# A diffusion layer's FFN stage: gate 2's rows in two f32r passes, columns summed by squares of 32 on VectorE, normed features moved by way of DRAM

## The chip, the cores and the metric

One core of a Trainium2 chip runs the whole layer in one launch. Its engines are TensorE (PE, matrix products and transposes into PSUM), VectorE (DVE), ScalarE (ACT), GpSimd (POOL) and SyncE (SP, which issues every DMA of this kernel). Each engine takes its instructions in a fixed order and waits on semaphores for the others. The metric is the time of one execution on the device, in microseconds (us).

## The reference

One layer over 256 latent tokens and 256 context tokens of width 2048. What matters here is the second half and the modulation that goes into it:

```python
sh1, sc1, g1, sh2, sc2, g2 = split(silu(c) @ w_ada + b_ada, 6)     # w_ada: 2048 x 12288
...
x = layer_norm(DN_ALPHA * x + g1 * (heads @ w_out), ln1_g, ln1_b)
u = x * (1 + sc2) + sh2
x = layer_norm(DN_ALPHA * x + g2 * ((silu(u @ w_gate) * (u @ w_up)) @ w_down), ln2_g, ln2_b)
```

w_gate and w_up are 2048 x 5632, w_down is 5632 x 2048, all f32. The 256 tokens are two tiles of 128 rows.

## The kernel before

**Products.** A large f32 product is made of three f32r products (mm3, lines 274 to 276): the weights are split into hi (an f32r copy by ACT, L264 or L498) and lo (raw minus hi by DVE, L265 or L501), the activations likewise, and hi x hi, lo x hi and hi x lo are summed. A 1 MB piece of weights lies in one of four raw buffers (load_raw, L244); it is split in two halves of 1024 columns, and four hi and four lo buffers hold them. A raw buffer comes free when DVE has made both lo halves, a hi or lo buffer when PE has used it.

**Modulations.** Most parts of silu(c) @ w_ada are summed on DVE: ada_vector_steps loads w_ada by pieces, and vector_sum (L384) adds each piece, times the value of c of its partition, into a tile adav of 128 partitions. What is left is the sum over the 128 partitions. Where the result is wanted as a row on all partitions (gate 2, g2sb), rows_from (L394) multiplies a 128x128 matrix of ones with the 512 columns in f32 and ACT copies the bank (L395). Where it is wanted as a column per feature (shift sh2 and scale sc2 of the second modulation), each 128 columns are the stationary side of an f32 matmul with two columns of ones (second_columns_of, L995, eight for 512 shifts and 512 scales; second_scales, L1291, four for 512 scales). DVE then writes sh2 and sc2, and combine (L988 to L990, POOL) makes of them and of the layer norm's gain and shift the two columns mA and mB per feature.

The 16 feature blocks of 128 form four groups of four. Group 0 is summed on DVE and placed in the planned part; group 1's shifts are summed on PE (L1270) and its scales on DVE (scales, placed by second_scales); groups 2 and 3 are summed on DVE (side, second_modulation).

**Normed rows.** normalise (L1068, DVE) leaves (x - mean) times 1/deviation in xt, tokens on the partitions. The FFN's product wants features on the partitions. z_part (lines 1326 to 1337) does this for two feature blocks: four 128x128 transposes on PE (L1330), two ACT scalings by mA and mB out of PSUM into uf (L1334), an ACT copy to u2h (L1336), and a DVE subtraction to u2l (L1337). Group 0 goes by z_flip and z_rest (L1303, L1449 to L1452) for each token tile; groups 1, 2 and 3 take two z_part each.

**Order.** Up to the end of the first layer norm the order is planned by a small scheduler written in the kernel (Flow) and, with a stretch after it, lies in a hand-ordered region (manual_schedule): each engine takes the region's instructions in the order of the program. The stretch holds the first FFN products and ends with normalise for the column groups 1 to 3. After the region the compiler's scheduler orders each engine by what is ready, earlier code first; it may put later instructions into gaps of the region.

**The first half of the FFN.** There are 11 hidden blocks of 512. For the first ten the products over the early feature groups are made before the rest and kept in spill tiles: blocks 0 to 2 over group 0 (one step for gate and one for up), blocks 3 to 9 over groups 0 and 1 (two steps each). A step (project) is one 1 MB piece of weights and 24 matmuls. first_half lists the steps: steps 0 and 1 (block 0) lie in the region as first_products; step 2 is block 1's gate, step 3 its up, steps 4 and 5 block 2, step 6 block 3's gate over group 0, step 7 the same over group 1, and so on. The scales' steps are merged with steps 3 to 5; then group 1 is combined and placed (combine(1), z_part(4), z_part(6)); then the steps from 6 on are merged with side; the last two steps follow the placing of groups 2 and 3. After that every block is finished in turn over its missing groups, activated (activate), turned by DVE in squares of 32 x 32 (squares, L1375), put to a DRAM scratch by four DMAs of 64 KB (put, L1380), read back by one of 256 KB (get, L1385), which moves the squares across the partitions, and split (place). The down projection follows, with gate 2's rows merged into it: ada_rows is used by gate2_steps, once per 512 columns.

## Time and profile before

| | |
|---|---|
| median of 3 runs | 1145.33 us (1141.98, 1145.33, 1145.77) |
| the profiled execution | 1143.35 us |
| its span, first to last instruction | 1141.5 us |
| granted TensorE clock, mean | 0.996 |
| instructions | 14234 |
| DMA | 321.28 MB, mean 281 GB/s |

Times of the trace are counted from the span's start. The FFN's first product starts at 396, the placing of group 1 lies at 432 to 439, that of groups 2 and 3 at 579 to 586, and gate 2's first row at 912. In lists of groups a line reads: line, engine, operation, output<-inputs, shapes, count | busy us, mean ns of one | idle time of the engine before them and what ended it. In the chain and the timeline a line reads: start, length, what, with the idle time before it in brackets. An f32 matmul shows as two records, an f32r matmul as one. "busy" of PE overlaps from one matmul to the next, since they are pipelined.

### The profile page before, as it was taken

The numbers are of one execution on the slowest core, as the hardware profiler recorded it, in microseconds if no ns is written. First come the engines' busy times: TensorE is split into PE (matmuls) and PEld (weight loads), VectorE is DVE, ScalarE is ACT, GpSimd is POOL, SyncE is SP. The second block draws the span as 40 slices with busy tenths as digits, with TensorE's granted clock in tenths as the row PEclk, the third lists the DMA queues.
The fourth block names the chain that finished last, engine by engine and source line by source line (L and its number), as shares of the span: only waits on it lengthen the run. The fifth ranks groups of instructions, "written<-read, shape, count | busy, mean of one in ns | idle before, by whom it ended". The sixth has DMA issues, their size and how long they took to land.

```text
span 1141.5 us, 14234 instructions
## 1 busy us (share of the span) xinstructions
PE 1120.3 (98%) x5347; PEld 905.3 (79%) x5347; DVE 829.0 (73%) x1053; ACT 546.6 (48%) x784; POOL 41.8 (4%) x82
## 2 busy tenths in 40 slices
PE   8999999999999999999999999999999999999995
PEld 8766678787878788888888888888888888888884
DVE  4753579899998897767767566776766787676556
ACT  3332454886784355444464444444444344333341
POOL 1000040110100000010000000000000000000000
PEclk9999999999999999999999999999999999999998
DMA  8999999786999878989876776677677888877531
GB/s 266 393 359 404 389 374 343 256 269 211 344 343 366 314 268 318 328 302 316 306 213 228 232 240 226 220 252 258 207 263 239 312 313 332 318 272 261 197 131 74
DMA packets 186270, 321.28 MB, mean 281 GB/s; under 512 B 8620, under 2 KB 51020, under 8 KB 183895
## 3 DMA queue, kind: packets, MB, share of 16 engines
q1 hardware_dynamic: 186200, 320.36, 80.7%
q8 instruction: 42, 0.69, 0.2%
q14 instruction: 28, 0.23, 0.1%
HBM read 304.07 MB, written 16.25 MB: 281 GB/s over the span
## 4 chain that ended last, share of the span: by engine, by line
PE 93%; DVE 4%; DMA 1%; ACT 1%; issue 1%; SPq 0%; DVEq 0%; ACTq 0%
PE acc L274 28%; PE acc L276 27%; PE acc L275 27%; PE wk L549 2%; PE wk L942 2%; DMA raw<-in_w_ada_dram 1%; PE wk L1133 1%; DVE g1b L384 1%; PE wk L274 1%; PE wk L276 1%; PE wk L275 1%; PE wk L636 1%; PE wk L995 0%; DVE lo L501 0%; DVE xt L1537 0%
## 5 line engine op out<-in xcount | busy, mean ns | idle before, releaser
L265 DVE TENSOR_TENSOR lo<-raw,hi 128x1024 fp32r<-128x1024 f32 x258 | 312.3, 1220 | 184.2 <-ACT hi L264 180.9
L264 ACT CAST hi<-raw 128x1024 fp32r<-128x1024 f32 x258 | 271.0, 1055 | 343.5 <-PE acc L276 302.6
L274 PE MATMUL acc<-hi,u2h 128*128 128x512 f32 x704 | 274.6, 390 | 1.4 <-ACT u2h L1451 1.4
L276 PE MATMUL acc<-hi,u2l 128*128 128x512 f32 x704 | 274.1, 389 | 0.0
L275 PE MATMUL acc<-lo,u2h 128*128 128x512 f32 x704 | 274.0, 389 | 0.0
L274 PEld LDWEIGHTS acc<-hi,u2h 128*128 128x128 f32 x704 | 132.2, 188 | 29.6 <-ACT u2h L1451 2.3
L276 PEld LDWEIGHTS acc<-hi,u2l 128*128 128x128 f32 x704 | 132.2, 188 | 27.9 <-DVE u2l L1452 0.6
L275 PEld LDWEIGHTS acc<-lo,u2h 128*128 128x128 f32 x704 | 132.2, 188 | 27.6 <-DVE lo L265 0.4
L498 ACT CAST hi<-raw 128x1024 fp32r<-128x1024 f32 (+1 forms) x86 | 87.4, 1031 | 120.0 <-DMA raw<-in_w_in_dram 58.7
L274 PE MATMUL acc<-hi,hTh 128*128 128x512 f32 x344 | 135.5, 394 | 0.0
L276 PE MATMUL acc<-hi,hTl 128*128 128x512 f32 x344 | 133.9, 389 | 0.0
L275 PE MATMUL acc<-lo,hTh 128*128 128x512 f32 x344 | 133.9, 389 | 0.0
L384 DVE SCALAR_TENSOR_TENSOR adav<-raw,cs,adav 128x512 f32<-128x512 f32 (+1 forms) x128 | 121.2, 947 | 10.8 <-DMA raw<-in_w_ada_dram 8.9
L501 DVE TENSOR_TENSOR lo<-raw,hi 128x1024 fp32r<-128x1024 f32 (+1 forms) x86 | 101.4, 1193 | 33.2 <-ACT hi L498 33.1
L274 PE MATMUL acc<-hi,uh 128*128 128x512 f32 x256 | 102.7, 401 | 0.4 <-DVE kvacc L701 0.3
L275 PE MATMUL acc<-lo,uh 128*128 128x512 f32 x256 | 100.0, 391 | 0.8 <-DVE lo L501 0.8
L276 PE MATMUL acc<-hi,ul 128*128 128x512 f32 x256 | 99.9, 390 | 0.0
L275 PEld LDWEIGHTS acc<-lo,hTh 128*128 128x128 f32 x344 | 64.6, 188 | 14.3 <-issue 1.0
L274 PEld LDWEIGHTS acc<-hi,hTh 128*128 128x128 f32 x344 | 64.6, 188 | 14.1 <-issue 1.0
L276 PEld LDWEIGHTS acc<-hi,hTl 128*128 128x128 f32 x344 | 64.6, 188 | 13.5
L274 PEld LDWEIGHTS acc<-hi,uh 128*128 128x128 f32 x256 | 48.1, 188 | 18.5 <-issue 5.9
L276 PEld LDWEIGHTS acc<-hi,ul 128*128 128x128 f32 x256 | 48.1, 188 | 10.3
(205 smaller groups left out, 1150.1 us busy)
## 6 DMA issues: line engine op xcount, KB each, us to landing
raw<-in_w_ada_dram SPq DMA_DIRECT2D x72, 1024.0 KB, 7.5
raw<-in_w_gate_dram SPq DMA_DIRECT2D x44, 1024.0 KB, 5.5
raw<-in_w_up_dram SPq DMA_DIRECT2D x44, 1024.0 KB, 5.2
raw<-in_w_down_dram SPq DMA_DIRECT2D x44, 1024.0 KB, 4.9
raw<-in_w_ada_dram SPq DMA_DIRECT2D x48, 512.0 KB, 6.8
raw<-in_w_in_dram SPq DMA_DIRECT2D x18, 1024.0 KB, 8.2
raw<-in_w_out_dram SPq DMA_DIRECT2D x16, 1024.0 KB, 7.8
pd<-hx SPq DMA_DIRECT2D x64, 128.0 KB, 2.6
```

Of the source, the lines that this page charges most:

```text
L264: nc.scalar.copy(hi[:, :n], raw[:, s : s + n])
L265: nc.vector.tensor_tensor(lo[:, :n], raw[:, s : s + n], hi[:, :n].bitcast(F32), op=ALU.subtract)
L274: nc.tensor.matmul(ps, lhsT=xh, rhs=w[0], start=first, stop=False, skip_group_check=seeded)
L275: nc.tensor.matmul(ps, lhsT=xh, rhs=w[1], start=False, stop=False, skip_group_check=seeded)
L276: nc.tensor.matmul(ps, lhsT=xl, rhs=w[0], start=False, stop=last, skip_group_check=seeded)
L384: nc.vector.scalar_tensor_tensor(a[:, c : c + piece], raw[:, f : f + piece], cs[:, 4 * (g * (G4 * NB // w) + j) + 2, None], a[:, c : c + p ...
L498: nc.scalar.copy(hl.hi[:, :n], raw.t[:, s : s + n])
L501: nc.vector.tensor_tensor(hl.lo[:, :n], raw.t[:, s : s + n], hl.hi[:, :n].bitcast(F32), op=ALU.subtract)
L549: nc.tensor.matmul(bank.t[32 * j : 32 * j + 32, :width], lhsT=cs[:, 4 * k + 2 - 2 * i : 4 * k + 34 - 2 * i], rhs=raw.t[:, c * width : (c + ...
L636: nc.tensor.transpose(ps.t[:, (j * 2 + t) * P : (j * 2 + t + 1) * P], src, ident)
L942: nc.tensor.matmul(o_ps.t[:, : 2 * P].rearrange("p (g q) -> p g q", q=32), lhsT=v, rhs=pv[:, k], start=k == 0, stop=k == 3)
L1133: nc.tensor.matmul(wps, lhsT=ident, rhs=ident, start=True, stop=True)
```

## The change

Four things are changed.

- The matrix of ones is made as f32r by an ACT instruction (0 times ident plus 1) and not by a POOL memset, and a table fold (128 x 32, a 1 where the partition modulo 32 is the column) is added, summed from the identity on DVE.
- Gate 2's rows: the 512 sums are split into an f32r part and its rest (split_rows: a copy on ACT, a subtraction on DVE), and two f32r matmuls with ones_r add both up (add_rows). Gate 1's rows are left as they were.
- Second modulation's columns, for group 1's scales and for groups 2 and 3: DVE transposes the adav tile in squares of 32 x 32 (one instruction for 512 columns) and sums each square's rows over 32 elements. This leaves, for each 32 columns, four partial sums on different partitions; four f32 matmuls with fold (32 stationary columns, 4 or 8 moving ones, each to 32 partitions of the bank) add them (fold_parts). Only one column is written to sh2 and sc2 where there were two equal ones. Group 0 and group 1's shifts are left as they were.
- Normed rows of groups 1, 2 and 3: instead of PE's transposes, DVE turns them by squares right behind normalise, still in the region, into the tiles of the last spills (z_squares: two instructions per group); SP puts them to DRAM by four DMAs per token tile (z_puts) and reads them back into the place of u2h by one per tile (z_gets); four ACT scalings read this with strides into two uf tiles, and then come the same copies and subtractions (z_place). Group 1's puts stand between steps 2 and 3, its gets after step 3; those of groups 2 and 3 are merged into the first fifth of the steps that follow step 5. z_place stands where z_part stood.

```diff
--- before.py
+++ after.py
@@ -328,8 +328,11 @@
 
     sel = main.tile([P, 4], F32, tag="sel", name="sel")
     nc.vector.reduce_sum(sel, ident.rearrange("p (j s) -> p s j", j=4)[:, 0:4, :], axis=AX.X)
-    ones = main.tile([P, P], F32, tag="ones", name="ones")
-    nc.gpsimd.memset(ones, 1.0)
+    fold = main.tile([P, 32], F32, tag="fold", name="fold")
+    nc.vector.reduce_sum(fold, ident.rearrange("p (a i) -> p i a", a=4), axis=AX.X)
+    ones_r = main.tile([P, P], F32R, tag="ones", name="ones")
+    nc.scalar.activation(ones_r, ident, AF.Copy, bias=1.0, scale=0.0)
+    ones = ones_r.bitcast(F32)
 
 
     bcol = main.tile([P, 6 * KD], F32, tag="bcol", name="bcol")
@@ -388,6 +391,14 @@
     def vector_sums(width):
         return main.tile([P, 2 * NB], F32, tag="adav", name="adav")[:, :width]
 
+    def split_rows(pair, src):
+        nc.scalar.copy(pair[0], src)
+        nc.vector.tensor_tensor(pair[1], src, pair[0].bitcast(F32), op=ALU.subtract)
+
+    def add_rows(ps, pair):
+        nc.tensor.matmul(ps, lhsT=ones_r, rhs=pair[0], start=True, stop=False)
+        nc.tensor.matmul(ps, lhsT=ones_r, rhs=pair[1], start=False, stop=True)
+
     def rows_from(sb, dst, s):
 
         ps = wk_bank()
@@ -397,7 +408,11 @@
     def ada_rows(c0, dst, sums):
         def done(sb):
             for s in range(0, dst.shape[-1], NB):
-                rows_from(sb, dst, s)()
+                pair = [pb.tile([P, NB], F32R, tag="t2k", name="rowpair", bufs=4) for _ in range(2)]
+                split_rows(pair, sb[:, s : s + NB])
+                ps = wk_bank()
+                add_rows(ps, pair)
+                nc.scalar.copy(dst[:, s : s + NB], ps)
 
         return ada_vector_steps((c0,), dst.shape[-1], sums, done)
 
@@ -589,6 +604,13 @@
         a = F.add("ACT", 60 + 0.9 * width, copy, [prev], [sb], [bank])
         b = F.add("PE", 224 * ncol, sums, [a], [ps], [sb])
         return a, [F.add("DVE", 160, lambda i=i: add(i), [b], give=[ps]) for i in range(2)]
+
+    def fold_parts(ps, part, n):
+
+        pv = part.rearrange("p s (j r) -> p s j r", r=4)
+        for r in range(4):
+            nc.tensor.matmul(ps[32 * r : 32 * r + 32, : pv.shape[1] * n].rearrange("p (s j) -> p s j", j=n), lhsT=fold,
+                             rhs=pv[:, :, :, r], start=True, stop=True)
 
     u = {}
 
@@ -996,6 +1018,22 @@
                              start=True, stop=True)
         return ps
 
+    def columns_by_squares(sb, n):
+
+        ps = wk_bank()
+        part = pb.tile([P, 1, n * 4], F32, tag="part", name="part", bufs=2)
+        for s in range(0, n * P, NB):
+            turned = pb.tile([P, NB], F32, tag="t2k", name="turned", bufs=4)
+            nc.vector.transpose(turned, sb[:, s : s + NB])
+            nc.vector.reduce_sum(part[:, 0, s // 32 : (s + NB) // 32], turned.rearrange("p (b j) -> p b j", j=32), axis=AX.X)
+        fold_parts(ps, part, n)
+        return ps[:, :n, None]
+
+    def place_columns(g, pv):
+        ks = slice(g * 4, g * 4 + 4)
+        nc.vector.tensor_copy(sh2[:, ks, 0:1], pv[:, 0:4])
+        nc.vector.tensor_scalar_add(sc2[:, ks, 0:1], pv[:, 4:8], 1.0)
+
     def second_place(g, ps):
         ks = slice(g * 4, g * 4 + 4)
         pv = ps[:, 0:16].rearrange("p (j s) -> p j s", s=2)
@@ -1004,7 +1042,7 @@
 
     def second_modulation(g, sums):
         def done(sb):
-            second_place(g, second_columns_of(sb))
+            place_columns(g, columns_by_squares(sb, 8))
             combine(g)
 
         return ada_vector_steps((3 * D + g * NB, 4 * D + g * NB), NB, sums, done)
@@ -1286,10 +1324,7 @@
         nc.vector.tensor_tensor(sh2[:, 4:8, :], pv[:, :, 0, :], bs, op=ALU.add)
 
     def second_scales(sb):
-        ps = wk_bank()
-        for j in range(4):
-            nc.tensor.matmul(ps[:, 2 * j : 2 * j + 2], lhsT=sb[:, j * P : (j + 1) * P], rhs=ones[:, 0:2], start=True, stop=True)
-        nc.vector.tensor_scalar_add(sc2[:, 4:8, :], ps[:, 0:8].rearrange("p (j s) -> p j s", s=2), 1.0)
+        nc.vector.tensor_scalar_add(sc2[:, 4:8, 0:1], columns_by_squares(sb, 4), 1.0)
 
 
 
@@ -1323,18 +1358,35 @@
     hTh = [pb.tile([P, 4, SEQ], F32R, tag=f"hTh{f}", name="hTh") if f < KF // 4 - SPLIT_F else None for f in range(KF // 4)]
     hTl = [pb.tile([P, 4, SEQ], F32R, tag=f"hTl{f}", name="hTl") if f < KF // 4 - SPLIT_F else None for f in range(KF // 4)]
 
-    def z_part(kk):
-        ps = wk_bank()
-        for j in range(2):
-            for t in range(NT):
-                nc.tensor.transpose(ps[:, (j * 2 + t) * P : (j * 2 + t + 1) * P],
-                                    xt[:, t, (kk + j) * P : (kk + j + 1) * P], ident)
-        uf = pb.tile([P, 2, SEQ], F32, tag="t2k", name="uf2", bufs=4)
-        for j in range(2):
-            nc.scalar.activation(uf[:, j, :], ps[:, j * SEQ : (j + 1) * SEQ], AF.Identity,
-                                 bias=mB[:, kk + j : kk + j + 1], scale=mA[:, kk + j : kk + j + 1])
-        nc.scalar.copy(u2h[:, kk : kk + 2, :], uf)
-        nc.vector.tensor_tensor(u2l[:, kk : kk + 2, :], uf, u2h[:, kk : kk + 2, :].bitcast(F32), op=ALU.subtract)
+    def z_squares(n):
+        for t in range(NT):
+            squares(xt[:, t, n * NB : (n + 1) * NB], spills[SPLIT_F - n][0][:, t, :])
+
+    def z_puts(n):
+        zd[n] = [put(spills[SPLIT_F - n][0][:, t, :]) for t in range(NT)]
+
+    def z_home(n):
+        return u2h[:, 4 * n : 4 * n + 4, :].bitcast(F32).rearrange("p q s -> p (q s)").rearrange("p (t x) -> p t x", t=NT)
+
+    def z_gets(n):
+        for t in range(NT):
+            get(zd[n][t], z_home(n)[:, t, :])
+
+    def z_place(n):
+        hv = z_home(n).rearrange("p t (a q i) -> p q t a i", a=4, q=4)
+        ufs = []
+        for q in range(0, 4, 2):
+            uf = pb.tile([P, 2, SEQ], F32, tag="t2k", name="uf2", bufs=4)
+            for j in range(2):
+                k = 4 * n + q + j
+                nc.scalar.activation(uf[:, j, :].rearrange("p (t a i) -> p t a i", t=NT, a=4), hv[:, q + j], AF.Identity,
+                                     bias=mB[:, k : k + 1], scale=mA[:, k : k + 1])
+            ufs.append(uf)
+        for uf, k in zip(ufs, (4 * n, 4 * n + 2)):
+            nc.scalar.copy(u2h[:, k : k + 2, :], uf)
+            nc.vector.tensor_tensor(u2l[:, k : k + 2, :], uf, u2h[:, k : k + 2, :].bitcast(F32), op=ALU.subtract)
+
+    zd = {}
 
     def residual_base(n):
 
@@ -1482,16 +1534,20 @@
     for n in range(1, 4):
         for t in range(NT):
             normalise(n, t)
+        z_squares(n)
     region.__exit__(None, None, None)
     run(first_half[2:3])
-    run(merge(first_half[3 : 2 * ONE_F], scales))
+    z_puts(1)
+    run(first_half[3:4])
+    z_gets(1)
+    run(merge(first_half[4 : 2 * ONE_F], scales))
     combine(1)
-    z_part(4)
-    z_part(6)
+    z_place(1)
     cutoff = len(first_half) - 2
-    run(merge(first_half[2 * ONE_F : cutoff], side))
-    for kk in range(EARLY_G * 4, KD, 2):
-        z_part(kk)
+    moves = [lambda n=n, f=f: f(n) for n in range(EARLY_G, ng) for f in (z_puts, z_gets)]
+    run(merge(first_half[2 * ONE_F : cutoff], side, moves + [lambda: None] * len(side)))
+    for n in range(EARLY_G, ng):
+        z_place(n)
     run(first_half[cutoff:])
     flips = []
```

## The prediction

> **What bounds the kernel now.** I read the page first: busy time by engine (part 1) and the shares of the chain that ended last (part 4).
>
> ```profile
> PE 1120.3 (98%) x5347; PEld 905.3 (79%) x5347; DVE 829.0 (73%) x1053; ACT 546.6 (48%) x784; POOL 41.8 (4%) x82
> ...
> PE 93%; DVE 4%; DMA 1%; ACT 1%; issue 1%; SPq 0%; DVEq 0%; ACTq 0%
> ```
>
> TensorE (PE) is busy for 98% of the span and holds 93% of the chain. So a microsecond (us) that PE no longer issues is a microsecond of the kernel, unless PE then waits; and each new wait of PE is paid in full. Second, the windows by stage (busy time of PE, PEld, DVE, ACT, POOL with their instruction counts, then clock, DMA share, GB/s), for the two stretches that hold the moved work.
>
> ```profile
> 405.00:433.00 28.00, 28.00 (x132) 23.40 (x132) 25.42 (x32) 15.74 (x21) 0.59 (x1) 1.00 0.83 311
> ...
> 530.00:582.00 52.00, 52.00 (x247) 43.55 (x247) 34.26 (x34) 26.00 (x33) 1.47 (x3) 1.00 0.84 293
> ```
>
> PE is full in both. VectorE (DVE) is busy for 25.4 of 28 us in the first, just after the FFN has begun, but for 34 of 52 in the second. The first is the place to watch. Third, the PE timeline (start, duration) there:
>
> ```profile
> 409.64 0.39 PE L274 MATMUL acc<-hi,u2h 128*128 128x512 f32 x1
> 409.87 0.39 PE L275 MATMUL acc<-lo,u2h 128*128 128x512 f32 x1
> ```
>
> Successive matmuls start 0.23 us apart, though each lasts 0.39: PE's price is the distance of starts. One FFN step of 24 matmuls is 24 x 0.2275 = 5.46 us. The row at 409.64 opens step 2 of the first half: 48 products for block 0 end just before it.
>
> **What PE loses.** The chain in order of time (start, length, what) gives the removed groups.
>
> ```profile
> 431.56 0.79 PE wk L1291 x8
> 432.35 0.93 PE wk L1330 x8
> ...
> 498.90 1.68 PE wk L995 x16
> 500.58 0.35 PE acc L274
> ...
> 571.47 1.68 PE wk L995 x16
> ...
> 578.76 1.75 PE wk L1330 x16
> ```
>
> Each f32 matmul has two records. The 24 transposes (L1330) cost 0.93 + 1.75 = **2.7 us** and go altogether. A set of eight column matmuls (L995) costs 1.68 plus 0.12 by which the next matmul is late (0.35 against 0.23): 1.80; two sets go (the third, at 387, stays). The four of L1291 cost 0.79 + 0.12 = 0.91.
>
> In the place of each set come four fold matmuls of 32 weight columns over 4 or 8 columns, eight records. No row shows them. The nearest are the 32-column matmuls of the first modulation, four column groups side by side:
>
> ```profile
> 10.49 1.01 PE wk L549 x32
> ```
>
> That is 0.03 us a record, so 0.25 a call; a record of L995, 1.68/16 = 0.105, gives 0.84 as the upper end. I take 0.4, near the first, whose weights have this width, with 0.12 for the change. Saved: 2 x (1.80 - 0.4) + (0.91 - 0.4) = **3.3 us** (2.0 to 3.8).
>
> Does the change of tile width itself cost? The chain has four transposes between 32-column matmuls (first row) and four between full ones (second row):
>
> ```profile
> 393.41 0.59 PE wk L1303 x4
> ...
> 401.10 0.63 PE wk L1303 x4
> ```
>
> They cost the same. The Trainium skill ("TensorEngine Tiling (Array Packing)", Key Properties) says that changing the tiling mode drains TensorE. By that rule each fold would lie near its upper end and the whole saving be 1.3 us smaller; the trace shows no such drain, so I keep 0.4.
>
> The four rows of gate 2 (L394), from the PE timeline:
>
> ```profile
> 911.97 0.40 PE L276 MATMUL acc<-hi,hTl 128*128 128x512 f32 x1
> 912.21 1.02 PE L394 MATMUL wk<-adav,ones 128*128 128x512 f32 x2
> 912.66 0.80 PE L274 MATMUL acc<-hi,hTh 128*128 128x512 f32 x1
> 913.30 0.39 PE L275 MATMUL acc<-lo,hTh 128*128 128x512 f32 x1
> ```
>
> From 911.97 to 913.30 there are 1.33 us; less two ordinary starts of 0.23 leaves 0.87 for one f32 row. Two f32r passes are two ordinary starts, 0.46. Saved: 4 x 0.41 = **1.6 us** (0, if f32r with ones were no faster, to 1.7). PE loses 2.7 + 3.3 + 1.6 = **7.6 us** in all (4.7 to 8.2).
>
> **What is added beside PE, and what hides it.** Durations of the groups nearest to the new DVE work:
>
> ```profile
> L1375 DVE STREAM_TRANSPOSE spill<-spill 128x512 f32<-128x512 f32 x20 | 13.0, 685 | 0.0
> L892 DVE TENSOR_REDUCE m<-wk 128x1 f32<-128x512 f32 x32 | 21.1, 675 | 1.1 <-PE wk L276 0.5 <-PE wk L885 0.4
> ```
>
> A set of 1024 columns takes two of each, 2.7 us of DVE between the last sum and the fold. Last sums today (DVE timeline, with the PE row of gate 2 that follows its sums soonest):
>
> ```profile
> 490.77 1.28 DVE L384 SCALAR_TENSOR_TENSOR adav<-raw,cs,adav 128x1024 f32<-128x1024 f32 x1
> ...
> 560.22 1.28 DVE L384 SCALAR_TENSOR_TENSOR adav<-raw,cs,adav 128x1024 f32<-128x1024 f32 x1
> ...
> 934.78 3.12 DVE L384 SCALAR_TENSOR_TENSOR adav<-raw,cs,adav 128x512 f32<-128x512 f32 x4
> ...
> 940.31 1.02 PE L394 MATMUL wk<-adav,ones 128*128 128x512 f32 x2
> ```
>
> The first two end 6.9 and 10.0 us before PE's columns at 498.90 and 571.47: hidden, at nothing; with that cover gone it would be 2.7 each. Gate 2's split (a copy on ACT, a subtraction on DVE of 0.6 to 0.7 each) has 2.4 us where it is tightest, 937.9 to 940.31, and is hidden too. Making ones on ACT and the fold table on DVE costs nothing: it lies in the start, whose first input is awaited from DMA:
>
> ```profile
> 1.64 1.76 DMA brow<-in_b_ada_dram
> ```
>
> Now the six transposes of the normed rows (z_squares). They stand in the hand-ordered region ahead of all later DVE work, with 6 x 0.685 = 4.1 us. DVE today:
>
> ```profile
> 400.87 2.32 DVE L384 SCALAR_TENSOR_TENSOR adav<-raw,cs,adav 128x512 f32<-128x512 f32 x3
> ...
> 404.70 2.83 DVE L1068 TENSOR_SCALAR xt<-xt,mv,ly 128x512 f32<-128x512 f32 x6
> 407.45 1.21 DVE L265 TENSOR_TENSOR lo<-raw,hi 128x1024 fp32r<-128x1024 f32 x1
> 408.59 0.74 DVE L384 SCALAR_TENSOR_TENSOR adav<-raw,cs,adav 128x512 f32<-128x512 f32 x1
> ```
>
> The lo part of step 2 is made right behind the normalising, ends at 408.66, and PE uses it at 409.87: a lead of 1.2 us. It cannot be earlier, since its hi waits for buffers that block 0's products free:
>
> ```profile
> 405.74 1.05 ACT L264 CAST hi<-raw 128x1024 fp32r<-128x1024 f32 x1 [1.30 <-PE acc L276]
> ...
> 414.54 1.05 ACT L264 CAST hi<-raw 128x1024 fp32r<-128x1024 f32 x1 [3.02 <-DMA raw<-in_w_gate_dram]
> ```
>
> With 4.1 us ahead of it lo ends at 412.8, and PE stands for **2.9 us** in step 2. Bounds: 0, if lo is put before the transposes, to 4.1. I take 2.9, because everything in the region is ready and stands earlier in the program.
>
> The moves are 24 puts and 6 gets on SP, the queue that also loads the weights (the first row's last number is its median to landing; the others are the puts that the kernel has already):
>
> ```profile
> raw<-in_w_gate_dram SPq DMA_DIRECT2D x44, 1024.0 KB, 5.5
> ...
> L1380 SPq DMA_DIRECT2D hd<-spill x80: 303/450/1352, 626.7 to 848.6; - x80
> ...
> DMA to landing us min/median/max: 1.6/5.0/5.9
> ```
>
> Eight puts of block 1 issue in 8 x 0.45 = 3.6 us from about 407 and land some 5 us later, near 415.5; its gets wait for that on SP, and the load of step 4's weights may stand behind them. Today that load is awaited already (the 3.02 at 414.54). In the new kernel a buffer comes free near 414, after the two lo of step 2 (411.6 + 2 x 1.2). Issued then, it lands (5.5) and is split (1.05 + 1.2) by 421.8; behind the gets, at 416, by 423.8. PE starts step 4 at 409.64 + 2 x 5.46 + 2.9 = 423.5 and uses lo 0.2 later. So nothing to 1 us is lost; I take 0.4, for gets that come first and a put or two that lands late. The other blocks' moves come later, when ACT waits for PE and not for data: nothing.
>
> Last, block 1's columns lead to u2h by sc, three POOL operations, four scalings, a copy and a split of step 7's weights. Today:
>
> ```profile
> 432.41 0.96 POOL L361 MEMSET adav<- 128x1024 f32 x1 [27.43 <-PE wk L1291]
> ...
> 434.27 1.48 ACT L1334 ACTIVATE uf<-wk,mB,mA 128x256 f32<-128x256 f32 x3 [2.08 <-POOL mB L990]
> 435.63 0.62 ACT L1336 CAST u2h<-uf 128x512 fp32r<-128x512 f32 x1
> ...
> 437.69 1.23 DVE L265 TENSOR_TENSOR lo<-raw,hi 128x1024 fp32r<-128x1024 f32 x1 [0.71 <-ACT hi L264]
> ...
> 438.97 0.50 PE L275 MATMUL acc<-lo,u2h 128*128 128x512 f32 x1
> ```
>
> Step 7's second matmul is late by 0.2 us already, for that lo. In the new order a fourth scaling comes before the first copy (+0.5), the memset no longer stands in POOL's way (-0.8), and PE arrives 1.3 us sooner (0.93 + 0.5 shorter): lateness grows by **0.3** (0 to 1).
>
> Sum: -7.6 + 2.9 + 0.4 + 0.3 = **-4.0 us**. The profiled execution took 1143.35 us with a span of 1141.5, so it would take 1139.4. The median of the three runs (1145.33; 1141.98 to 1145.77) lies 2 us above; the four times centre near 1144.1. I forecast 1140.5.
>
> **Rivals.** (1) *The start is not hurt*: DVE makes lo before the transposes, or PE finds other work. For it: later work is put into DVE's gaps (the L384 at 400.87 is of that kind). Against it: no gap is left between 404.7 and 411.6. It gives -7.6 + 0.6 = -7 us: 1137.5. (2) *PE's saving is small*: folds at 0.84 and f32r rows at no gain take 2.9 us off the saving, the start is as forecast: -1 us, 1143.5. (3) *Slower: SP's queue.* If the gets of block 1 are held longer on SP, the loads of steps 4 and 5 and the sums' loads wait behind them at a time when nothing is stored up. It decides from an issue of the gets near 416; each us later is a us of PE. To end 3.5 us slower it has to be 7.5 us later, at 423, by waits on the puts of 12 us and not 5: 1149. For it speaks that DMA is 0.83 busy there; against it the longest landing of such puts, 5.9.
>
> **How the numbers follow.** About 0.3% (3.4 us) is what a measurement of this kernel can tell from no change. Chances: forecast 0.5; no hurt 0.17; small saving 0.21; SP 0.12. The forecast lies at -0.35%, near that bound, so of its half 0.38 is faster and 0.12 the same; with rival 1 faster has 0.55, with rival 2 the same has 0.33, slower 0.12. The range for 8 in 10 goes from rival 1 with its best saving, 1136.5, to above rival 2, 1145.5; SP's case and some noise stay out.
>
> **What would show it.** Right: no L1330, L1291 and only one early L995; eight short records per fold; the rows of gate 2 as pairs 0.23 apart; six transposes behind the normalising, and PE waiting some 3 us for lo (L265's line) near 410. Wrong: PE without a wait there (rival 1), fold groups over 0.8 us (rival 2), or hi waiting for the gate's DMA over 5 us with SP held by the gets (rival 3). A wait of PE for a fold at 499 or 571 would break the hiding by DVE.

## The result: slower by 0.4%, and the profile after

The changed kernel takes 1149.51 us (median of 6 runs, 1147.28 to 1150.26) against 1143.67 for the kernel before in the same comparison (6 runs, 1141.98 to 1145.77): ratio **1.0042** [1.0027, 1.0056]. The forecast was 1140.5, its range up to 1145.5. The profiled execution took 1149.55 us, span 1147.8 us, mean clock 0.994.

The page after, parts 1 and 4 (busy time; shares of the chain):

```profile
PE 1117.6 (97%) x5307; PEld 899.2 (78%) x5307; DVE 837.8 (73%) x1074; ACT 548.7 (48%) x789; POOL 41.5 (4%) x81
...
PE 84%; DVE 8%; DMA 5%; issue 2%; ACT 1%; SPq 0%; POOL 0%; DVEq 0%; POOLq 0%; ACTq 0%
```

PE's busy time fell by 2.7 us only, and its share of the chain went from 93% to 84%, with more of the chain on DVE (8% for 4%) and on DMA (5% for 1%). The work that PE was to lose it did lose. PE's timeline after:

```profile
437.28 0.24 PE L612 MATMUL wk<-part,fold 128*32 128x4 f32 x8
...
920.08 0.40 PE L399 MATMUL wk<-rowpair,ones 128*128 128x512 f32 x1
920.32 0.40 PE L400 MATMUL wk<-rowpair,ones 128*128 128x512 f32 x1
920.56 0.40 PE L274 MATMUL acc<-hi,hTh 128*128 128x512 f32 x1
```

A fold set takes 0.24 us for its eight records (0.4 was taken), and a row of gate 2 takes 920.56 - 920.08 = 0.48 us where it took 0.87 (0.46 was taken). No transposes of groups 1 to 3 are left.

Where the time went is seen by laying the two traces side by side: the start of the same matmul after, less its start before.

| place (time before, us) | after - before, us | what lies between |
|---|---|---|
| 40 | +2.0 | the start |
| 385 | +3.4 | first half of the layer |
| 420 | +5.3 | step 2 waits for lo |
| 433 | +3.7 | group 1's transposes and column matmuls gone |
| 438.6 | +6.0 | steps 6 and 7 |
| 439.0 | +8.9 | step 7's lo |
| 440.7 | +9.8 | matmuls at half the pace |
| 444.6 | +12.4 | step 8's hi and lo |
| 500.4 | +11.1 | group 2's columns gone |
| 573.0 | +9.7 | group 3's columns gone |
| 580.6 | +7.9 | groups 2 and 3's transposes gone |
| 1062.9 | +6.7 | gate 2's rows shorter |

So three things cost: about 3 us before the FFN, 1.9 us in step 2, and 8.7 us from 433 to 445. PE's waits after, from 400 to 600 us (engine, line <- what released it: us in total, times, longest):

```profile
PE acc L275 <- DVE lo L265: 5.0, 4, 2.5
PE acc L274 <- ACT hi L264: 1.9, 2, 1.0
PE acc L274 <- ACT u2h L1503: 1.4, 1, 1.4
```

Before, the same view had one line:

```profile
PE wk L1303 <- DVE xt L1068: 0.3, 1, 0.3
```

The wait for u2h is not new. It is that of group 0, which came just before 400 then, with the same 1.4 us. The first of the lo waits is the one forecast, of 1.15 us: four hi products of step 2 went ahead of it. DVE's timeline after:

```profile
409.02 1.29 DVE L1427 STREAM_TRANSPOSE spill<-xt 128x512 f32<-128x512 f32 x2
...
413.23 1.29 DVE L1427 STREAM_TRANSPOSE spill<-xt 128x512 f32<-128x512 f32 x2
414.45 4.58 DVE L265 TENSOR_TENSOR lo<-raw,hi 128x1024 fp32r<-128x1024 f32 x4
...
444.04 2.60 DVE L387 SCALAR_TENSOR_TENSOR adav<-raw,cs,adav 128x1024 f32<-128x1024 f32 x2
446.56 2.35 DVE L265 TENSOR_TENSOR lo<-raw,hi 128x1024 fp32r<-128x1024 f32 x2
```

Step 2's lo begins only when the six squares are done. Step 7's lo, at 446.56, stands behind two sums. ACT's timeline after, at the same place (in brackets the idle time before, and what ended it):

```profile
443.51 1.99 ACT L264 CAST hi<-raw 128x1024 fp32r<-128x1024 f32 x2 [0.19 <-DMA raw<-in_w_gate_dram]
454.06 0.59 ACT L1488 COPY spill<-acc 128x512 f32<-128x512 f32 x1 [8.55 <-PE acc L276]
454.54 1.05 ACT L264 CAST hi<-raw 128x1024 fp32r<-128x1024 f32 x1
```

ACT makes step 7's hi at 443.51, when its piece of weights lands; that was issued at 436.60 (424.67 before), and group 1's scalings stand ahead of the hi until 443.3. Then ACT stands for 8.55 us in front of a copy of finished banks, which waits for PE to end step 7, and the hi of step 8, which PE wants next, stands behind that copy. PE and ACT wait for each other in turn. ACT's timeline before has the last half of step 7's hi and both of step 8's ahead of that copy:

```profile
438.06 2.96 ACT L264 CAST hi<-raw 128x1024 fp32r<-128x1024 f32 x3
443.84 0.59 ACT L1436 COPY spill<-acc 128x512 f32<-128x512 f32 x1 [2.81 <-PE acc L276]
```

PE's waits from 436 to 458 have more than one cause. 0.8 us are for step 6's lo, which stands behind the columns' transpose and sum on DVE; 1.0 for step 7's hi, whose weights come late; 2.5, the longest, for step 7's lo behind the two sums; 0.9 and 0.5 for step 8's hi and lo, behind the copy on ACT. Step 8's weights had landed at 450.2, 3.9 us before that copy began.

Last, the windows after (busy time of each engine, then granted clock, DMA share, GB/s):

```profile
442.00:445.00 3.00, 1.99 (x10) 1.28 (x8) 2.17 (x3) 2.78 (x5) 0.00 (x0) 1.00 1.05 386
445.00:448.00 3.00, 0.51 (x3) 0.17 (x2) 2.96 (x4) 0.51 (x1) 0.00 (x0) 0.99 1.06 388
448.00:451.00 3.00, 3.00 (x8) 2.33 (x9) 2.96 (x3) 0.00 (x0) 0.00 (x0) 0.50 1.00 327
451.00:454.00 3.00, 3.00 (x14) 2.46 (x13) 0.43 (x1) 0.00 (x0) 0.00 (x0) 0.94 0.81 213
```

After the waits for step 7's hi and lo, with two matmuls between them, PE's clock falls to 0.50 for 3 us and then recovers: 0.5 x 3 + 0.06 x 3 = **1.7 us** lost on top of the waits. A full window of eight matmuls instead of fourteen is the sign of it. Before, the clock was 1.00 in all windows from 20 to 1062 us.

### The profile page after: what moved, and what is told of

Its sections match the earlier page's. It is cut to its first block, busy times and chain, and to the rows that moved or that the text cites. A ratio compares the mean times of both kernels' runs of the same rounds, so it can differ in the third digit from the quotient of the medians.

```text
span 1147.8 us, 14212 instructions
## 1 busy us (share of the span) xinstructions
PE 1117.6 (97%) x5307; PEld 899.2 (78%) x5307; DVE 837.8 (73%) x1074; ACT 548.7 (48%) x789; POOL 41.5 (4%) x81
## 4 chain that ended last, share of the span: by engine, by line
PE 84%; DVE 8%; DMA 5%; issue 2%; ACT 1%; SPq 0%; POOL 0%; DVEq 0%; POOLq 0%; ACTq 0%
PE acc L275 25%; PE acc L274 25%; PE acc L276 25%; DMA raw<-in_w_ada_dram 3%; PE wk L564 2%; PE wk L964 2%; DVE g1b L387 1%; DMA raw<-in_w_in_dram 1%; DVE adav L387 1%; DVE lo L265 1%; PE wk L1171 1%; DVE lo L516 1%; PE wk L274 1%; PE wk L276 1%; PE wk L275 1%
## 5 line engine op out<-in xcount | busy, mean ns | idle before, releaser
L275 PEld LDWEIGHTS acc<-lo,uh 128*128 128x128 f32 x256 | 48.1, 188 | 10.7 <-DVE lo L516 1.7
```

Of the source, the lines that this page charges most:

```text
L275: nc.tensor.matmul(ps, lhsT=xh, rhs=w[1], start=False, stop=False, skip_group_check=seeded)
```

## The experiments

Ratios are to the kernel before, run on the same chip, with 95% intervals. "the filler" is an unused tile of 416 bytes per partition in the pool main, which comes before the raw buffers.

### The parts one by one

**rows_columns**: the changed kernel with z_part and its calls put back (rows in two passes, columns by squares, new start; no moves).

> The gate-2 rows and the columns by squares as in the changed kernel, the normed rows by PE's transposes as before. Queue theory (the loss comes from the moves: puts on SP that hold back weight loads, and the DVE transposes ahead of lo): PE saves 1.6 for the rows and 3.3 for the columns and loses no more than 0.5 in new waits, so 4 to 5 us below the kernel before (about 1139.5 on 1143.7). Rival (the columns' DVE transposes and sums, put ahead of lo, are what makes PE wait between 430 and 455): no gain or a loss of 2 to 5 us, with PE waiting for lo near 435. If the 3.4 us that the changed kernel is late before 390 come from the new start (ones on ACT, fold on DVE), this kernel has them too and ends only 1 to 2 us faster.

**moves_alone**: the kernel before with the moves only.

> The kernel before with only the normed rows moved by way of DRAM. Queue theory: transposes save 2.7 us, the DVE transposes in the region cost 2.3 to 2.9, the puts on SP 6 to 8, so 6 to 8 us slower than before (about 1151). Rival (columns): about the kernel before, within 1 us. Its start is that of the kernel before: if the first 390 us take 3 us longer here too, the new start is not their cause.

**start_alone**: the kernel before with the change's first hunk only (fold and ones).

> The kernel before with only the new start: ones made by ACT as f32r, fold summed on DVE, no memset on POOL; nothing uses fold. If the start is the cause of the 3.4 us by which the changed kernel is late before 390: 3 us slower than before, with the delay growing at the first weight loads (13 to 60 us). If that delay is only how the loads ran in that execution: the kernel before within 1 us.

**moves_late**: the changed kernel, the moves of groups 2 and 3 put off to about 500 us.

```diff
-    run(merge(first_half[2 * ONE_F : cutoff], side, moves + [lambda: None] * len(side)))
+    run(merge(first_half[2 * ONE_F : cutoff], side, [lambda: None] * 8 + moves + [lambda: None] * 8))
```

> The changed kernel with the puts and gets of groups 2 and 3 put off from the first fifth of the merged steps to the middle (near 500 us), where weights are stored ahead. Queue theory: the wait of steps 6 to 9 for their weights goes, some 5 to 7 us of the 7.5 come back: 1143 to 1145; a part stays if 7 to 10 us of held queue are more than what is stored ahead. Rival (columns ahead of lo): no change against the changed kernel, 1149.5.

| run | median, us | ratio |
|---|---|---|
| rows_columns | 1142.13 | 0.9984 [0.9969, 0.9999] |
| moves_alone | 1151.39 | 1.0058 [1.0042, 1.0075] |
| start_alone | 1146.24 | 1.0024 [1.0012, 1.0036] |
| moves_late | 1152.52 | 1.0071 [1.0051, 1.0091] |

The moves are the loss, and the start is a second one of nearly 3 us: the trace of moves_alone lies within 0.4 us of before up to 409, start_alone's is 2.5 us late at 400. moves_late was a miss: its lag behind the kernel before grew by 4.6 us and not 8.6 from 433 to 446, but by another 5.4 up to 520, where the moves now were.

### The start: is it where the buffers lie?

fold takes 128 bytes per partition and pushes all later tiles by as much. **start_pad** is start_alone, **rows_columns_pad** rows_columns, with the filler cut by those 128 bytes; **pad_only** is the kernel before with the filler grown by them; **after_pad** is the changed kernel with the filler cut. The edit (in pad_only the new number is 544):

```diff
-    fill(main, 416)
+    fill(main, 288)
```

> start_alone with the filler tile ahead of xt made 128 bytes per partition smaller (416 to 288), so that fold no longer moves every later tile by 128 bytes; the order of the first instructions is that of start_alone. Address theory (packets to the moved raw buffers take 98 ns and not 84, 32 and not 27, since the buffers' addresses are 128 bytes off): within 0.1% of the kernel before, some 2.8 us below start_alone, the packet times back. Rival (the order on POOL: ident ready at 3.0 us and not at 1.4, PE's warm-up late): no change against start_alone, 1146.2.

> rows_columns with the same smaller filler. Address theory: the 4.9 us that PE saves by the rows and the columns are seen in full but for small new waits: 4 to 5 us below the kernel before, about 1139, ratio 0.996. Rival (POOL's order): as rows_columns, 1142.

> The kernel before with nothing but the filler tile made 128 bytes per partition larger (416 to 544), which moves the later tiles by as much as fold does. Address theory: as start_alone, 0.2 to 0.3% slower (about 1146.4), with packets of 98 and 32 ns in the first 35 us. If the order on POOL had a share in it, less than that.

> The changed kernel with the filler 128 bytes smaller, so that the buffers lie as in the kernel before. Address theory: 2.5 to 3.4 us below the changed kernel, about 1146.5, ratio to before 1.002; what is left, some 7 us above rows_columns_pad, is the price of the moves. If it stays at 1149.5, the two causes are not additive.

| run | median, us | ratio |
|---|---|---|
| start_pad | 1143.26 | 0.9992 [0.9981, 1.0004] |
| rows_columns_pad | 1139.12 | **0.9955** [0.9941, 0.9968] |
| pad_only | 1146.14 | 1.0008 [0.9993, 1.0023] |
| after_pad | 1146.66 | 1.0022 [1.0007, 1.0037] |

The window from 8 to 35 us, when all DMA engines are busy and the kernel waits for data: before, start_alone, start_pad, pad_only, in that order.

```profile
8.00:35.00 27.00, 27.00 (x299) 23.18 (x297) 12.87 (x23) 11.12 (x22) 0.00 (x0) 1.00 1.00 327
```

```profile
8.00:35.00 27.00, 27.00 (x283) 23.70 (x286) 12.34 (x21) 10.21 (x20) 0.00 (x0) 1.00 0.99 301
```

```profile
8.00:35.00 27.00, 27.00 (x292) 23.52 (x295) 12.50 (x22) 10.64 (x21) 0.00 (x0) 1.00 1.00 324
```

```profile
8.00:35.00 27.00, 26.66 (x284) 22.78 (x283) 12.41 (x23) 10.75 (x21) 0.00 (x0) 1.00 1.00 302
```

The DMA engines are equally full, but move 327, 301, 324 and 302 GB/s. The packets themselves are slower: from 8 to 14 us the median 512-byte packet takes 27, 32, 27 and 32 ns, the 2048-byte one 84, 98, 84 and 98. So the place of the buffers alone slows the early loads (pad_only has it with none of the change's instructions), and with the place restored the new start costs nothing that can be told (start_pad). For the end of the kernel pad_only is less clear: 1.0008 overlaps start_alone's 1.0024 and also no change. With the filler cut the rows and columns bring 0.45%, 5.1 us, against 4.9 forecast for them.

The Trainium skill ("DMA: Bandwidth & Descriptors", How a descriptor splits into AXI transactions) says that a transfer is cut into pieces of 256 bytes from 256-byte boundaries, so that one that starts off a boundary needs a piece more. That a shift by 128 bytes slows packets agrees in kind, but not in size: by that rule a 512-byte packet needs three pieces for two and a 2048-byte one nine for eight (an estimate from the rule), while both grew by nearly the same share here, 32/27 and 98/84. No trace here shows the addresses, so the reason stays open.

### What holds the moves?

First theory: SP. In the changed kernel puts of group 2 wait on SP, and the weights of step 7 stand behind them. SP's waits after (380 to 700 us):

```profile
SPq L1432 <- DMA raw<-in_w_gate_dram: 4.0, 2, 2.8
...
SPq L1432 <- DMA raw<-in_w_up_dram: 2.4, 1, 2.4
```

A put reads nothing of these loads. But the program's DMAs signal eight semaphores in turn, and a waiting put waits for its own semaphore, last signalled by the DMA issued eight before it (the put at 434.55 went 0.02 us after the gate piece issued at 427.25 had landed, at 434.53). **moves_spread** issues one put or get at a time, spread over the steps (its last put of group 3 reads a spill tile after block 7's copy has written it, so a part of group 3's features is not moved):

```diff
...
-    moves = [lambda n=n, f=f: f(n) for n in range(EARLY_G, ng) for f in (z_puts, z_gets)]
+    moves = sum(([lambda n=n, t=t, a=a: z_put(n, t, a) for t in range(NT) for a in range(4)]
+                 + [lambda n=n, t=t: get(zd[n][t], z_home(n)[:, t, :]) for t in range(NT)] for n in range(EARLY_G, ng)), [])
...
```

**squares_later** takes the squares of groups 2 and 3 out of the region, to behind step 3:

```diff
-        z_squares(n)
+        if n == 1:
+            z_squares(n)
     region.__exit__(None, None, None)
...
     z_gets(1)
+    for n in range(EARLY_G, ng):
+        z_squares(n)
```

> The changed kernel with the 16 puts and 4 gets of groups 2 and 3 handed out one for each step of the first half, and not eight puts in a row. Queue theory (each put waits on SP for the landing of the DMA issued eight before it, so eight puts in a row hold SP for 7 to 10 us and the weights behind them come late): a put then waits for DMAs long landed, the 5 to 6 us lost between 438 and 455 come back but for the part of group 1: 1143 to 1145. Rivals: the bytes that the moves add (1.5 MB each way) or DVE's columns ahead of lo are the cost: no change, 1149.

> The changed kernel with the four DVE transposes of groups 2 and 3 put behind step 3 and no longer in the region; those of group 1 stay. Theory of the delayed lo: the 2.3 us that PE waits near 412 fall to 0.5 or less, and 1.5 to 2 us come back (1147.5), if nothing behind takes them. Rival: the wait is taken over by the late weights of steps 4 to 7, which the held queue sets anyway: no change, 1149.5.

| run | median, us | ratio |
|---|---|---|
| moves_spread | 1155.24 | 1.0093 [1.0078, 1.0109] |
| squares_later | 1149.60 | 1.0046 [1.0031, 1.0061] |

Both missed. In moves_spread no put waited for a landing any more, and it was the slowest of all: it lost 9 us from 433 to 445 as the changed kernel did, and more at 501, 517 and 544. Its end is no test of the theory, since its last put stood on SP for 10.6 us, up to 548.8, for block 7's copy; the stretch up to 445 is. In squares_later step 2 lost only 0.2 us, but step 5, at 426, lost 4.1 (waits of 1.6 and 0.5 us, then the half clock). ACT's timeline of moves_spread shows what stayed:

```profile
455.42 0.59 ACT L1494 COPY spill<-acc 128x512 f32<-128x512 f32 x1 [8.49 <-PE acc L276]
455.90 1.05 ACT L264 CAST hi<-raw 128x1024 fp32r<-128x1024 f32 x1
```

Again the copy stands ahead of step 8's hi. ACT's order is fixed before the run, by a scheduler that orders by when it thinks things are ready.

**group1_moved** and **group23_moved** are rows_columns_pad with group 1 alone, or groups 2 and 3 alone, moved; the others keep z_part. In group1_moved:

```diff
...
+        if n == 1:
+            z_squares(n)
...
-    z_part(4)
-    z_part(6)
+    z_place(1)
```

> rows_columns_pad with only group 1 moved by way of DRAM (its two squares in the region, eight puts, two gets, placing by strides); groups 2 and 3 by PE's transposes. Theory A (the start of the FFN has nothing stored up, so what delays lo, the loads of steps 4 to 7 and the placing of group 1 is paid): 3 to 5 us above rows_columns_pad (1142 to 1144), with PE's waits at steps 2, 6 and 7. Theory B (the sixteen puts of groups 2 and 3 are the price, wherever they stand, as moves_late and moves_spread suggest): within 1 us of rows_columns_pad.

> rows_columns_pad with only groups 2 and 3 moved (four squares in the region, sixteen puts and four gets where the changed kernel has them); group 1 by PE's transposes. Theory A: the lo of step 2 is some 1.5 us late, the rest is hidden but for the held queue: 0 to 3 us above rows_columns_pad less the 1.75 of the transposes saved. Theory B: 4 to 6 us above rows_columns_pad (1143 to 1145), with PE waiting at steps 7 and 8 where ACT has the copy of the finished banks ahead of the next hi.

| run | median, us | ratio |
|---|---|---|
| group1_moved | 1146.89 | 1.0021 [1.0006, 1.0035] |
| group23_moved | 1141.85 | 0.9981 [0.9967, 0.9995] |

Against rows_columns_pad group 1 costs 0.66% (7.5 us), with eight puts and two gets; groups 2 and 3 cost 3.0 us. They do not add up (after_pad: 7.7). ACT's timeline of rows_columns_pad, then of group1_moved:

```profile
421.46 1.27 ACT L1471 COPY spill<-acc 128x512 f32<-128x512 f32 x2 [2.46 <-PE acc L276]
422.62 2.00 ACT L264 CAST hi<-raw 128x1024 fp32r<-128x1024 f32 x2
426.90 1.27 ACT L1471 COPY spill<-acc 128x512 f32<-128x512 f32 x2 [2.28 <-PE acc L276]
```

```profile
419.58 1.27 ACT L1501 COPY spill<-acc 128x512 f32<-128x512 f32 x2 [3.00 <-PE acc L276]
425.02 1.26 ACT L1501 COPY spill<-acc 128x512 f32<-128x512 f32 x2 [4.17 <-PE acc L276]
426.18 2.00 ACT L264 CAST hi<-raw 128x1024 fp32r<-128x1024 f32 x2
```

In the first the hi casts of step 5 come behind the copies of step 3, in the second behind those of step 4: one step later, after 4.17 us of idleness. Step 5's weights had landed at 422.95, 2.1 us before these copies, so ACT waited by its order and not for data. PE's timeline of group1_moved has the price:

```profile
427.28 0.73 PE L274 MATMUL acc<-hi,u2h 128*128 128x512 f32 x2 [1.62 <-ACT hi L264]
428.54 0.72 PE L275 MATMUL acc<-lo,u2h 128*128 128x512 f32 x1 [0.52 <-DVE lo L265]
429.05 0.63 PE L276 MATMUL acc<-hi,u2l 128*128 128x512 f32 x1
429.48 0.63 PE L275 MATMUL acc<-lo,u2h 128*128 128x512 f32 x1
```

1.62 + 0.52 us of waiting, and then matmuls 0.43 us apart and not 0.23, until 432: the half clock again. This execution took 1143.09 us, 3.8 less than the median of its kernel, and from 409 on it loses 5.1 us to the trace of rows_columns_pad; what made most others longer is not in it.

### An order written by hand

Second theory: the moves change the order that the scheduler gives to ACT and to SP's loads, and this is the price. **hand** is rows_columns_pad with ACT's order from step 4 on written out: the hi casts of a step follow the copies of the step two before it (earlies loads and splits, first_half multiplies and copies). Only ACT's order is fixed by hand; but the loads and the lo parts are written in the same place as the casts, so the scheduler gives SP and DVE another order too. **hand_group1** and **hand_all** have the same order with group 1, or all groups, moved.

```diff
+    def unit(i):
+        first_half[i]()
+        if i + 2 < cutoff:
+            earlies[i + 2]()
...
+    hand = tc.manual_schedule(engines={ET.Activation})
+    hand.__enter__()
+    run(earlies[4:6])
+    run(merge([units[4], units[5]], scales))
```

> The control: the rows in two passes, the columns by squares, the filler of 288 and no moves (PE transposes place all groups); from step 4 on ACT's order is written out by hand: the hi parts of the next step but one behind the copies of each finished step, those of step 7 ahead of group 1's scalings. As the kernel with the same parts and the scheduler's own order measured 1139.1 us (0.9955), I expect 0.9955 within 0.002 under either theory; if the order by hand costs something of its own, it shows here.

> The same order of ACT by hand, with group 1 alone moved by way of DRAM. Theory A (order): in the kernel with group 1 alone moved, ACT's order, fixed before the run, has the hi parts of step 5 one step later, behind the copies of step 4, where ACT stands idle for 4.2 us; the waits of PE that follow (3.6 us in the trace), and the stretch of half the clock behind them (some 1.7 us each), are the price. With ACT's order as in the control, it ends within 2.5 us of the control (ratio of the two below 1.0025). Theory B (data): the loads themselves come late, by the puts and gets on SP's queue and by DMA; then ACT's order changes nothing and it ends 5 to 7.5 us above the control.

> The same order of ACT by hand, with groups 1, 2 and 3 moved as in the changed kernel. Theory A: within 2.5 us of the control, at best 1 us below it, since 2.7 us of PE's transposes are gone. Theory B: 5 to 8 us above the control, as with the scheduler's order (7.5).

| run | median, us | ratio |
|---|---|---|
| hand | 1148.14 | 1.0042 [1.0030, 1.0055] |
| hand_group1 | 1150.36 | 1.0062 [1.0045, 1.0078] |
| hand_all | 1149.99 | 1.0055 [1.0042, 1.0068] |

The control itself lost 9 us. The moves add 0.20% and 0.13% to it, which lies within theory A's 2.5 us; but with so much lost already the three decide little. PE's waits of hand say where:

```profile
PE acc L274 <- ACT u2h L1371: 4.1, 1, 4.1
PE wk L612 <- DVE part L1028: 3.6, 2, 3.2
```

The loads for group 1's last sums now stood behind those of later weights, PE waited for the fold and then for u2h, all at one place (440), with 0.66 of the clock in the window from 440 to 450. **sums_first** mends that: each piece of the sums goes ahead of the weights of one step, as it was. **sums_first_all** adds all moves, and **sums_first_late** writes the squares of groups 2 and 3 after group 1's placing (z_place(1)), no longer in the region.

```diff
-    run(first_half[3:4])
+    run([scales[0], first_half[3]])
...
-    run(earlies[4:6])
-    run(merge([units[4], units[5]], scales))
+    run([scales[1], earlies[4], scales[2], earlies[5], scales[3], units[4], units[5]])
```

> The control hand lost 9 us to the kernel with the scheduler's own order, all of it at 440: the loads for the scales' sums came behind those of later steps, so PE waited 3.2 us for the columns and 4.1 us for group 1's features, and the clock was halved for a while; before and after that place it lost nothing. Here the four pieces of the scales' sums are each put ahead of the weights of steps 3, 4, 5 and 6, as they were. No moves, ACT's order by hand. I expect 0.9955 within 0.002 (1138 to 1141); if it stays above 1.000 the order by hand has another price, and the two kernels below say less.

> The same with groups 1, 2 and 3 moved as in the changed kernel. Sum from rows of hand_all: against the control, 2.4 us for the six squares ahead of step 2's lo, less 1.4 us at 579 and 1.3 us at 440 for the transposes, up to 1.6 us for later lo parts. Theory A (the moves' price is the order of ACT and SP that they bring about, and the half clock behind PE's waits): 0 to 2.5 us above the control, 1138 to 1143, ratio 0.995 to 0.999. Theory B (the moves' own traffic and issues): 5 to 8 us above the control, ratio 1.000 to 1.003.

> The same as the kernel before it, with the squares of groups 2 and 3 written after group 1's placing, so that two squares and not six stand ahead of step 2's lo. Theory A: the wait in step 2 falls from 2.4 to about 1 us and nothing takes its place, so 1 to 1.5 us below the kernel before it, ratio 0.994 to 0.998. Theory B, or the squares found to be in the way of the sums later: no change, or worse.

| run | median, us | ratio |
|---|---|---|
| sums_first | 1139.50 | 0.9960 [0.9944, 0.9977] |
| sums_first_all | 1140.90 | 0.9973 [0.9956, 0.9989] |
| sums_first_late | 1138.84 | **0.9955** [0.9938, 0.9972] |

The control is back, and the moves now cost 1.5 us (0.9973 - 0.9960), which these intervals don't tell from nothing, where they cost 7.7. The interval of sums_first_all lies wholly below that of after_pad, which has the same work, the same 24 puts and 6 gets among it, in the scheduler's order. So the bytes and the issues of the moves are not the main price. PE's waits of sums_first_all (400 to 600 us), then its ACT and DVE timelines and its window at the place of the loss, with the changed kernel's window last:

```profile
PE acc L275 <- DVE lo L265: 1.7, 2, 1.2
PE acc L274 <- ACT u2h L1386: 1.3, 1, 1.3
...
PE acc L274 <- ACT hi L264: 0.3, 1, 0.3
```

```profile
433.50 2.01 ACT L264 CAST hi<-raw 128x1024 fp32r<-128x1024 f32 x2
...
440.49 2.00 ACT L264 CAST hi<-raw 128x1024 fp32r<-128x1024 f32 x2
445.21 1.27 ACT L1488 COPY spill<-acc 128x512 f32<-128x512 f32 x2 [2.72 <-PE acc L276]
...
433.76 3.49 DVE L265 TENSOR_TENSOR lo<-raw,hi 128x1024 fp32r<-128x1024 f32 x3
```

```profile
436.00:460.00 24.00, 22.71 (x101) 18.47 (x100) 16.15 (x16) 13.27 (x18) 1.22 (x2) 1.00 0.96 338
```

```profile
436.00:460.00 24.00, 18.25 (x76) 13.34 (x75) 16.24 (x17) 12.19 (x17) 2.48 (x4) 0.93 0.98 342
```

The waits for lo and hi fell from 6.9 to 2.0 us, with a new one of 1.3 for group 1's features, and the clock stays at 1.00 there (0.93 in the changed kernel). Step 7's hi (433.50) now comes ahead of group 1's scalings, step 8's (440.49) ahead of the copy, and step 7's lo (in the DVE line) ahead of the sums. The weights of steps 5 and 7 are issued 10.0 and 18.8 us after the first put (13.3 and 26.9 in the changed kernel), step 7's now ahead of group 2's puts, which wait for landings as they did (the one at 435.29 for the piece issued at 427.37). The orders of ACT, DVE and SP were changed together, so what each is worth alone is not told apart. With the squares later as well, step 2's wait shrinks and the kernel is 0.45% faster than before: as fast as rows_columns_pad without any moves, so the transposes' 2.7 us are just paid for by what the moves still cost.

## Why the prediction was wrong, point by point

- **PE's 7.6 us: right.** Rows and columns brought 5.1 us (rows_columns_pad), 4.9 forecast, a fold set 0.24 us, a row 0.48; no drain was seen at the folds. The transposes of groups 2 and 3 left 1.75 us at 580, as summed.
- **Step 2's lo, +2.9: right in kind, too large.** The lag grew by 1.9 us, by the order given. PE did four hi products while lo was made, so it stood for 1.15 only.
- **Step 4's load behind the gets, +0.4: about right.** The gets were issued at 413.68 and 417.34 (416 expected), and PE had no wait from 420 to 436. But this and step 7's 0.3 were all that was charged to group 1's puts, gets and placing, and moved alone group 1 cost 7.5 us. The third rival came near the time by luck (1149; 1148 on the base that its neighbours use): its gets were not held. SP was held, but later, by the puts of groups 2 and 3.
- **"The other blocks' moves come later, when ACT waits for PE and not for data: nothing": the step that failed.** ACT did wait for PE, but in front of a copy with the next step's hi behind it; and data came late as well, since group 2's eight puts took SP 7.2 us (427.66 to 434.85) ahead of step 7's weights. The price of added DMAs was looked for in their landing; it lay in the order of everything else on ACT, DVE and SP, which was taken from the trace of before as if it would stay. With the order by hand the moves' net price fell from 7.7 to 1.5 us (sums_first_all).
- **Step 7's chain, +0.3: failed with it.** A longer POOL and ACT chain was summed there. Of the loss of 5.2 us between 433 and 439, 4.3 are waits: 0.8 for step 6's lo behind the DVE work for group 1's columns (1.4 us, which the sum left out), 1.0 for step 7's hi, whose weights were issued 12 us later than before (5 of them the lag there already), and 2.5 for its lo behind two sums.
- **"Making ones on ACT and the fold table on DVE costs nothing": failed.** The instructions cost nothing (start_pad); their tile cost 2 to 4 us by moving the later tiles, the raw buffers among them (after against after_pad: 0.20%, 2.3 us; rows_columns against rows_columns_pad: 0.29%; start_alone against start_pad: 0.32%). A new tile was not counted as an edit.
- **"Each new wait of PE is paid in full": too little.** Waits close together can also halve the clock for some 3.4 us, which costs 1.7 us, or for twice that (moves_alone with 0.86 of the clock from 436 to 460, hand). Over all executions the mean clock was 0.996 before, 0.9935 after and 0.996 in sums_first_late (medians); 0.0025 of 1145 us is 2.9, an estimate from rounded numbers.

Sum as it came: -7.6 + 1.9 (step 2) + 2.3 (buffers) is -3.4. The measured +5.8 leaves 9.2 us for the order of ACT, DVE and SP and the half clock behind it; 0.7 was forecast for all that. Left open: what the three orders are worth singly, and why pad_only, with loads as slow as start_alone's, ends less clearly late.

## What to carry to other kernels

Where a scheduler orders the engines, an added DMA or a tile is not a local edit: compare the order of casts, copies, sums and loads around it, on every engine, with that of the kernel before, and hold that order by hand before the edit is judged. A small new tile can move every later buffer, so check the time of the same loads, or keep their places with a filler. Price a wait of PE by its neighbours too, since several short ones cost the clock as well.

## What the runs showed of the hardware

- PE's clock can halve after short waits. In group1_moved two waits of 1.62 and 0.52 us with 0.7 us of work between them were enough: 0.50 from 429 to 432. The Trainium skill ("TensorE: Matmul & The Clock Gate", What's actually happening) has a gate that looks at activity in windows of about 3.4 us and halves the clock after an idle one; length and depth of the slow stretch agree, and here a window with some work in it sufficed.
- A put's issue on SP waited for the landing of the DMA issued eight before it, 0.02 us after it where the trace gives the landing. The instructions of the trace show it as a wait for one of eight semaphores used in turn, so it is a wait of these programs; no run shows a limit of the queue itself.
- With the buffers moved by 128 bytes a 2048-byte packet took 98 ns and not 84 (8 to 14 us), and 301 GB/s were moved and not 327, with all DMA engines busy (8 to 35 us).
- A POOL multiplication took 1.18 us beside a DVE subtraction (438.46 to 439.70), and an addition of the same shape 0.20 us behind it; why is not shown. POOL's groups after, 434 to 460 us (count | busy us, mean ns):

```profile
L1011 POOL TENSOR_TENSOR mB<-lcol,sc 128x4 f32<-128x4 f32 x1 | 1.2, 1180 | 0.0
...
L1012 POOL TENSOR_TENSOR mB<-mB,sh 128x4 f32<-128x4 f32 x1 | 0.2, 200 | 0.1
```
